# A decoder block that streams its weights: pieces split three ahead, with two raw buffers and 28 units

## The chip, the cores and the metric

The kernel runs on one core of a Trainium2 chip. The metric is the device time of one execution, in microseconds (us). A core has a matrix engine (TensorE, PE in the profile, with PEld for its weight loads), VectorE (DVE), ScalarE (ACT), GpSimd (POOL) and SyncE (SP), and 16 DMA engines that move data between the main memory and the on-chip memory. Each engine works through its own instructions in order and waits for the others by semaphores. In the profile SPq is the queue on which SyncE issues transfers.

## The reference

One decoder block over 256 tokens of width 2048, in float32. Cut to what matters:

```python
h = rms_norm(x, g_mix)
proj = h @ w_in                       # retention, dilated attention and their gates
merged = sigmoid(gate_ret) * (ret @ w_br_ret) + sigmoid(gate_dil) * (dil @ w_br_dil)
x = x + merged @ w_out
x = x + memory_cross_attention(rms_norm(x, g_cross), rms_norm(mem, g_mem), w_q_mem, w_kv_mem, w_o_mem)
hf = rms_norm(x, g_ffn)
# PEER: 16 of 16384 experts for each of 8 heads and each token
a = gelu(einsum('td,tkd->tk', hf, peer_u[idx]))
x = x + einsum('tk,tkd->td', a * gates, peer_v[idx])
out = rms_norm(x, g_final)
```

## The kernel before

All weights come from the main memory as 464 pieces of 1 MiB (128 partitions x 4 x 512 floats), in one fixed order. Pieces 0 to 99 are `w_in`, then follow the weights of the branches, of the output, of the cross attention and of the expert queries up to piece 207; pieces 208 to 335 are the table `u` of the experts and pieces 336 to 463 the table `v`. The experts are not gathered for most tokens: for 192 of the 256 tokens the kernel multiplies with the whole tables, weighted by a gate matrix G that it builds in the main memory. For the other 64 tokens it gathers rows of `u` and `v` (`lanes`, line 835) and works on them with VectorE (lines 843 and 861).

A float32 product is made of three products of a rounded high part and a low part. So each piece is loaded into a raw buffer (line 1167, issued by SyncE), ScalarE rounds it to the high part `hi` (line 1177), and VectorE subtracts to get the low part `lo` (line 1178). TensorE then multiplies with `hi` and `lo` (`mm3`, lines 210 to 212, and lines 916, 917, 1026, 1027): 24 products of 512 columns for a piece up to 207, 20 for a later one.

The order of the instructions is the order of the program text; nothing is reordered. `ahead(n)` stands before the work on piece n and splits all pieces up to n + SPLIT_AHEAD; behind each split it issues the load that reuses the raw buffer just read. The high and low parts have three buffers each (pool `stream`), the raw pieces three (RAW_BUFS), so the parts of piece n + 2 go into the buffers of piece n - 1, and the raw piece i + 3 into the buffer of piece i.

All other work is cut into generators that advance by `tick()` between the products: transposes, attention, the choice of the experts, the gate matrix (`gate_matrix`), the gathered rows (`lanes`), and `weigh`, which loads the gate rows and activations of a chunk of experts five items ahead (lines 939 to 944, on the SP queue), multiplies them (VectorE, line 969), transposes them on TensorE (line 974), copies the high part out on ScalarE (lines 977, 981) and the low part on VectorE (lines 950, 955). `weigh` runs during the second half of the program.

Nearly everything else that is kept on chip lies in one pool `units` of 30 buffers of 4 KiB per partition: tiles of x, rows of activations, operands of the expert products, gathered rows. A new unit takes a free buffer and its first writer waits for the last reader of the tile that held it. The three pools that the change touches take 3 x 8 + 2 x 3 x 8 + 30 x 4 = 192 KiB per partition.

Of the kernel before, what the change touches and what calls it, by code (L numbers as in the profile page):

```python
# [20 lines left out]
KQ = 4  # L21
# [8 lines left out]
N_EXP = N_KEYS * N_KEYS  # L30
N_CH = N_EXP // 512
V_GROUPS = (4, 8, 8, 8, 4)
RAW_BUFS = 3
SPLIT_AHEAD = 2
N_UNITS = 30
LANES = slice(64, 128)
LOW = slice(0, 64)
TICK = 4.0
# [37 lines left out]
def block_kernel(ctx, tc, a, out):  # L76
    nc = tc.nc
    ctx.enter_context(tc.manual_schedule())
    cp = ctx.enter_context(tc.tile_pool(name="consts", bufs=1))
    st = ctx.enter_context(tc.tile_pool(name="stream", bufs=3))  # L80
    up = ctx.enter_context(tc.tile_pool(name="units", bufs=N_UNITS))
    wp = ctx.enter_context(tc.tile_pool(name="work", bufs=4))
    sp = ctx.enter_context(tc.tile_pool(name="small", bufs=2))
# [3 lines left out]
    def unit(shape, dt=F32):  # L87
        return up.tile([128] + shape, dt, tag="unit", name="unit")
# [83 lines left out]
    def split_sb(raw, gi, kq, ks=range(4), into=None):  # L172

        hi, lo = into or (unit([4, T], F32R), unit([4, T], F32R))
        for k in ks:
            g = gains[:, gi, 4 * kq + k:4 * kq + k + 1]
            nc.scalar.activation(hi[:, k], raw[:, k], AF.Copy, scale=g)
            nc.vector.scalar_tensor_tensor(lo[:, k], raw[:, k], g, hi[:, k], op0=OP.mult, op1=OP.subtract)
        return hi, lo
# [69 lines left out]
    x_T = [None] * KQ  # L249
    sm = {}  # L250

    def load_xT(kq):
        raw = unit([4, T])
        nc.sync.dma_start(raw, a["xT"][kq])
        return raw
# [899 lines left out]
    stream = [e for e in prog if e[0] is not None]  # L1155
# [3 lines left out]
    def quarters(i):  # L1159
        return [slice(k, k + 1) for k in range(KQ)] if i <= RAW_BUFS else [slice(0, KQ)]  # L1160

    def load_to(m):
        while at["load"] < min(m, len(stream)):
            i = at["load"]
            raws[i] = st.tile([128, KQ, 512], F32, name="raw", bufs=RAW_BUFS)
            for ks in quarters(i):
                nc.sync.dma_start(raws[i][:, ks], stream[i][0][:, ks])
            at["load"] += 1

    def ahead(n):  # L1170
        while at["split"] < min(n + SPLIT_AHEAD + 1, len(stream)):
            i = at["split"]
            load_to(i + RAW_BUFS)
            raw = raws.pop(i)
            hi, lo = st.tile([128, KQ, 512], F32R, name="hi"), st.tile([128, KQ, 512], F32R, name="lo")
            for ks in quarters(i):
                nc.scalar.copy(hi[:, ks], raw[:, ks])  # L1177
                nc.vector.tensor_sub(lo[:, ks], raw[:, ks], hi[:, ks])  # L1178
            parts[i] = (hi, lo)
            at["split"] += 1  # L1180
            load_to(i + 1 + RAW_BUFS)

    raw_x = []
    for i in range(RAW_BUFS):
        raw_x.append(load_xT(i))
        raws[i] = st.tile([128, KQ, 512], F32, name="raw", bufs=RAW_BUFS)
        for k in range(KQ):
            nc.sync.dma_start(raws[i][:, k], stream[i][0][:, k])
    at["load"] = RAW_BUFS
    raw_x.append(load_xT(3))  # L1190
    for i in range(RAW_BUFS):
        raw = raws.pop(i)
        hi, lo = st.tile([128, KQ, 512], F32R, name="hi"), st.tile([128, KQ, 512], F32R, name="lo")
# [6 lines left out]
        parts[i] = hi, lo  # L1200
        at["split"] = i + 1
        load_to(i + 1 + RAW_BUFS)
    x_T[3] = split_sb(raw_x[3], 0, 3)
    n = 0
    for ap, fn in prog:
        if ap is None:
# [99 lines left out]
```

## Time and profile before

| | us |
|---|---|
| runs shown: median of 3 (lowest to highest) | 2597.49 (2588.37 to 2598.75) |
| the profiled execution | 2592.94 |
| its span, from the first to the last instruction | 2591.0 |
| TensorE busy in the span | 2497.3 |
| VectorE busy | 1874.5 |
| ScalarE busy | 1256.3 |
| GpSimd busy | 553.0 |

The rows below are from the profiled execution. Times on the left of a row count from the start of the span. In a row of a group of instructions, what stands before the bar is the line, the engine, the operation, what is written and read, and the count; behind it are busy time and mean duration, then the engine's idle time just before these instructions and what ended most of it. TensorE's products overlap, so that one has a mean of 0.39 us though a new one starts every 0.23 us.

### The profile page before, as it was taken

How to read it: one execution, taken by the hardware profiler on the slowest of the kernel's cores; microseconds unless marked ns; L12 is line 12 of the kernel's file. 1: busy time of each engine (PE TensorE's matmuls, PEld its weight loads, DVE VectorE, ACT ScalarE, POOL GpSimd, SP SyncE). 2: the span in 40 equal slices, each digit the busy share in tenths (PEclk: the TensorE clock that was granted, in tenths of full speed). 3: DMA queues.
4: the chain of work that ended last, by engine and by line, in shares of the span. 5: the costliest groups of instructions: out<-in, count | busy, mean ns of one | idle time of the engine just before them, and what ended most of it. 6: DMA issues, size and time to landing. Idle time of an engine off the chain costs nothing.

```text
span 2591.0 us, 29643 instructions
## 1 busy us (share of the span) xinstructions
PE 2497.3 (96%) x11426; PEld 2062.8 (80%) x11426; DVE 1874.5 (72%) x2168; ACT 1256.3 (48%) x1302; POOL 553.0 (21%) x361
## 2 busy tenths in 40 slices
PE   9999999999999999999989989999999899998998
PEld 7888888888888888888867768887877787876886
DVE  7566545787564344456889998887779888898984
ACT  6434334443355443454544458885554344443444
POOL 0211110001100000000023332323334454443621
PEclk9999999999999999999999999999999999999999
DMA  8555555567666554465569889999999999999984
GB/s 293 193 182 169 189 187 176 190 212 268 211 241 214 183 176 145 164 216 175 200 236 357 303 287 342 361 355 359 383 357 376 348 403 357 400 385 343 380 344 154
DMA packets 160141, 700.50 MB, mean 270 GB/s; under 512 B 15968, under 2 KB 40576, under 8 KB 101120
## 3 DMA queue, kind: packets, MB, share of 16 engines
q1 hardware_dynamic: 110352, 531.18, 57.6%
q0 software_dynamic: 42736, 154.85, 15.7%
q10 hardware_dynamic: 6912, 12.59, 1.3%
q8 instruction: 89, 1.46, 0.2%
q14 instruction: 52, 0.43, 0.0%
HBM read 666.01 MB, written 31.98 MB: 269 GB/s over the span
## 4 chain that ended last, share of the span: by engine, by line
PE 65%; DVE 11%; DMA 6%; issue 2%; ACT 1%; POOL 0%; SPq 0%; ACTq 0%; DVEq 0%; POOLq 0%
PE acc L211 16%; PE acc L212 16%; PE acc L210 16%; DVE lo L1178 5%; PE acc L1026 3%; PE acc L1027 3%; PE acc L916 3%; PE acc L917 3%; DMA unit<-G 2%; DMA raw<-in_v_dram 2%; DVE unit L843 2%; PE sm L772 2%; DMA unit<-act 1%; PE tp L193 1%; PE sm L594 1%
## 5 line engine op out<-in xcount | busy, mean ns | idle before, releaser
L1178 DVE TENSOR_TENSOR lo<-raw,hi 128x2048 fp32r<-128x2048 f32 (+1 forms) x464 | 1059.5, 2285 | 534.5 <-ACT hi L1177 533.5
L1177 ACT CAST hi<-raw 128x2048 fp32r<-128x2048 f32 (+1 forms) x464 | 880.2, 1900 | 665.9 <-PE acc L212 288.8
L211 PE MATMUL acc<-lo,unit 128*128 128x512 f32 x2688 | 1055.9, 393 | 33.9 <-DVE lo L1178 33.1
L210 PE MATMUL acc<-hi,unit 128*128 128x512 f32 x2688 | 1065.6, 396 | 6.5 <-ACT hi L1197 6.5
L212 PE MATMUL acc<-hi,unit 128*128 128x512 f32 x2688 | 1052.2, 391 | 0.0
L211 PEld LDWEIGHTS acc<-lo,unit 128*128 128x128 f32 x2688 | 508.2, 189 | 148.2 <-DVE lo L1178 47.4
L210 PEld LDWEIGHTS acc<-hi,unit 128*128 128x128 f32 x2688 | 508.0, 189 | 107.8 <-ACT hi L1197 7.0
L212 PEld LDWEIGHTS acc<-hi,unit 128*128 128x128 f32 x2688 | 507.8, 189 | 105.5
L835 POOL DMA_INDIRECT unit<-in_u_rows_dram,unit x128 | 216.4, 1691 | 446.8 <-DVE unit L843 157.6
L835 POOL DMA_INDIRECT unit<-in_v_rows_dram,unit x128 | 230.6, 1801 | 253.6 <-DVE unit L861 161.9
L1026 PE MATMUL acc<-hi,unit 128*128 128x512 f32 x512 | 201.7, 394 | 0.0
L1027 PE MATMUL acc<-lo,unit 128*128 128x512 f32 x512 | 201.3, 393 | 0.0
L916 PE MATMUL acc<-hi,unit 128*128 128x512 f32 x512 | 201.0, 393 | 0.0
L917 PE MATMUL acc<-lo,unit 128*128 128x512 f32 x512 | 200.6, 392 | 0.0
L861 DVE SCALAR_TENSOR_TENSOR unit<-unit 128x1024 f32<-128x1024 f32 x128 | 161.9, 1279 | 7.2 <-DMA unit<-xs 6.7
L843 DVE CUSTOM_DVE_ANT_0 unit<-unit 128x1024 f32<-128x1024 f32 x128 | 155.8, 1218 | 0.7 <-DMA unit<-in_u_rows_dram,unit 0.5
L1026 PEld LDWEIGHTS acc<-hi,unit 128*128 128x128 f32 x512 | 97.5, 190 | 21.1 <-DVE unit L955 0.2
L1027 PEld LDWEIGHTS acc<-lo,unit 128*128 128x128 f32 x512 | 97.4, 190 | 20.8
L916 PEld LDWEIGHTS acc<-hi,unit 128*128 128x128 f32 x512 | 97.3, 190 | 20.9
L917 PEld LDWEIGHTS acc<-lo,unit 128*128 128x128 f32 x512 | 97.1, 190 | 20.9
L342 POOL TENSOR_TENSOR unit<-work 128x512 f32<-128x512 f32 x20 | 37.7, 1884 | 176.4 <-DVE work L340 157.1
L169 POOL TENSOR_TENSOR rstd<-rstd2t,nhalf 128x2 f32<-128x2 f32 x1 | 0.7, 695 | 338.2 <-DVE rstd2t L163 338.2
(235 smaller groups left out, 1437.6 us busy)
## 6 DMA issues: line engine op xcount, KB each, us to landing
raw<-in_u_dram SPq DMA_DIRECT2D x128, 1024.0 KB, 6.9
raw<-in_v_dram SPq DMA_DIRECT2D x128, 1024.0 KB, 8.1
raw<-in_w_in_dram SPq DMA_DIRECT2D x96, 1024.0 KB, 4.9
raw<-in_w_kv_dram SPq DMA_DIRECT2D x32, 1024.0 KB, 4.9
raw<-in_w_out_dram SPq DMA_DIRECT2D x16, 1024.0 KB, 4.9
raw<-in_w_qm_dram SPq DMA_DIRECT2D x16, 1024.0 KB, 4.9
raw<-in_w_om_dram SPq DMA_DIRECT2D x16, 1024.0 KB, 4.9
raw<-in_w_pq_dram SPq DMA_DIRECT2D x16, 1024.0 KB, 4.9
```

What stands on the lines that cost most here:

```text
L210: nc.tensor.matmul(acc, lh, rh, start=start, stop=False)
L211: nc.tensor.matmul(acc, lh, rl, start=False, stop=False)
L212: nc.tensor.matmul(acc, ll, rh, start=False, stop=stop)
L835: nc.gpsimd.indirect_dma_start(rows[i], None, t, bass.IndirectOffsetOnAxis(ap=ix[:, j // 2, j % 2:j % 2 + 1], axis=0))
L843: nc.vector.tensor_tensor_reduce(r, r, hn[i % 2].rearrange("p a b -> p (a b)"), 1.0, 0.0, OP.mult, OP.add, dots[:, i // 2, i % 2:i % 2 + 1])
L861: nc.vector.scalar_tensor_tensor(y, r, coef[:, i // 2:i // 2 + 1], y, op0=OP.mult, op1=OP.add)
L916: nc.tensor.matmul(accs[1], th[:, k, 128:256], hi[:, k], start=first, stop=False)
L917: nc.tensor.matmul(accs[1], th[:, k, 128:256], lo[:, k], start=False, stop=last)
L1026: nc.tensor.matmul(accs[n][1], tb[:, k], hi[:, k], start=f, stop=False)
L1027: nc.tensor.matmul(accs[n][1], tb[:, k], lo[:, k], start=False, stop=e)
L1177: nc.scalar.copy(hi[:, ks], raw[:, ks])
L1178: nc.vector.tensor_sub(lo[:, ks], raw[:, ks], hi[:, ks])
```

## The change

The high and low parts get four buffers each and are made three pieces ahead; the raw pieces get two buffers, and the pool of units 28. The three pools take 2 x 8 + 2 x 4 x 8 + 28 x 4 = 192 KiB per partition, as before. At the start, two pieces and two tiles of x are loaded in turn, then the other two tiles of x, and these two are split behind the first two pieces.

```diff
-RAW_BUFS = 3
-SPLIT_AHEAD = 2
-N_UNITS = 30
+RAW_BUFS = 2
+SPLIT_AHEAD = 3
+N_UNITS = 28
@@
-    st = ctx.enter_context(tc.tile_pool(name="stream", bufs=3))
+    st = ctx.enter_context(tc.tile_pool(name="stream", bufs=SPLIT_AHEAD + 1))
@@
     at["load"] = RAW_BUFS
-    raw_x.append(load_xT(3))
+    raw_x.extend(load_xT(i) for i in range(RAW_BUFS, KQ))
     for i in range(RAW_BUFS):
         raw = raws.pop(i)
         hi, lo = st.tile([128, KQ, 512], F32R, name="hi"), st.tile([128, KQ, 512], F32R, name="lo")
@@
-    x_T[3] = split_sb(raw_x[3], 0, 3)
+    for i in range(RAW_BUFS, KQ):
+        x_T[i] = split_sb(raw_x[i], 0, i)
     n = 0
     for ap, fn in prog:
```

## Rows read from the trace of the kernel before

**Rows 1.** Busy time of the engines by stretch: span, PE, PEld, DVE, ACT, POOL, clock, DMA share, GB/s.
```profile
65.00:1242.00 1177.00, 1175.61 (x5458) 980.23 (x5457) 678.51 (x655) 510.33 (x515) 90.82 (x85) 1.00 0.56 193
1242.00:1546.00 304.00, 272.39 (x1151) 215.26 (x1150) 285.39 (x546) 144.66 (x122) 74.45 (x44) 0.98 0.79 284
1546.00:1799.00 253.00, 246.66 (x1279) 210.75 (x1278) 207.73 (x334) 210.02 (x337) 67.75 (x42) 0.99 0.97 347
1799.00:1942.00 143.00, 140.88 (x622) 116.09 (x621) 113.55 (x109) 74.61 (x60) 51.37 (x30) 0.99 0.99 372
1942.00:2371.00 429.00, 396.10 (x1765) 321.89 (x1764) 375.21 (x329) 176.13 (x135) 187.10 (x106) 0.97 1.00 376
2371.00:2484.00 113.00, 113.00 (x502) 93.58 (x502) 101.56 (x70) 49.28 (x30) 66.27 (x35) 1.00 0.96 372
```
**Rows 2.** The same stretches, VectorE's subtractions of line 1178 alone: busy time and count.
```profile
65.00:1242.00 1177.00, 457.27 (x199) 1.00 0.56 193
1242.00:1546.00 304.00, 128.48 (x57) 0.98 0.79 284
1546.00:1799.00 253.00, 100.76 (x44) 0.99 0.97 347
1799.00:1942.00 143.00, 68.74 (x30) 0.99 0.99 372
1942.00:2371.00 429.00, 184.05 (x81) 0.97 1.00 376
```
**Rows 3.** Groups of TensorE's instructions, the whole span: the two with most idle time.
```profile
L211 PE MATMUL acc<-lo,unit 128*128 128x512 f32 x2688 | 1055.9, 393 | 33.9 <-DVE lo L1178 33.1
...
L974 PE MATMUL tp<-ident,unit 128*128 128x128 f32 x192 | 32.0, 292 | 31.4 <-DVE unit L950 20.9 <-DVE unit L955 5.9 <-DVE unit L969 4.6
```
**Rows 4.** Timeline of ScalarE, 2387 to 2403 us: start, duration, instruction, idle time before.
```profile
2387.59 1.92 ACT L1177 CAST hi<-raw 128x2048 fp32r<-128x2048 f32 x1 [2.62 <-PE acc L1026]
2392.12 1.91 ACT L1177 CAST hi<-raw 128x2048 fp32r<-128x2048 f32 x1 [2.62 <-PE acc L1026]
```
**Rows 5.** Timeline of VectorE, 2387 to 2403 us.
```profile
2385.11 2.29 DVE L1178 TENSOR_TENSOR lo<-raw,hi 128x2048 fp32r<-128x2048 f32 x1
2387.32 1.28 DVE L861 SCALAR_TENSOR_TENSOR unit<-unit 128x1024 f32<-128x1024 f32 x1
2389.54 2.29 DVE L1178 TENSOR_TENSOR lo<-raw,hi 128x2048 fp32r<-128x2048 f32 x1 [0.94 <-ACT hi L1177]
```
**Rows 6.** Timeline of the SP queue, 2387 to 2403 us: three issues, from the first on.
```profile
2387.43 9.29 SPq L1167 DMA_DIRECT2D raw<-in_v_dram  x3
```
**Rows 7.** Raw loads from 65, 1242, 1546, 1799, 2484 us to the next.
```profile
DMA to landing us min/median/max: 4.7/4.9/10.6
...
DMA to landing us min/median/max: 4.7/5.5/9.8
...
DMA to landing us min/median/max: 4.7/7.9/11.8
...
DMA to landing us min/median/max: 4.8/8.2/14.5
...
DMA to landing us min/median/max: 4.8/5.1/9.0
```
**Rows 8.** Two single raw loads, issued at 2403.7 and 1354.6 us.
```profile
DMA to landing us min/median/max: 5.1/5.1/5.1
...
DMA to landing us min/median/max: 8.7/8.7/8.7
```
**Rows 9.** What ended the idle time before the splits, 1799 to 2591 us: us, times.
```profile
  DMA raw<-in_v_dram: 98.3, 35
```
**Rows 10.** The row gathers of line 835, 1990 to 2500 us, and their engine's waits.
```profile
L835 POOL DMA_INDIRECT unit<-in_v_rows_dram,unit x128: 932/1737/3942, 2005.0 to 2484.5; - x128
...
  DVE unit L861: 161.9, 70
...
DMA to landing us min/median/max: 4.8/10.2/16.5
```

## The prediction

> **What bounds the kernel now.** I read the busy time by stage first [rows 1], with the number of splits in each stage [rows 2]; then what TensorE waits for [rows 3]; then one turn of the raw buffers on ScalarE, VectorE and the DMA queue [rows 4 to 6]; then how long the loads take in each stage [rows 7, 8]; last what ends the waits of the splits, and the row gathers [rows 9, 10].
>
> TensorE is the bound nearly everywhere. From 65 to 1242 us it is busy 1175.6 of 1177 us, and from 2371 to 2484 all the time. Its idle time lies in three stages [rows 1]: 304 - 272.4 = 31.6 us from 1242 to 1546, 253 - 246.7 = 6.3 us up to 1799, and 429 - 396.1 = 32.9 us from 1942 to 2371. Of all its idle time only 33.9 us end with a split that came late (the second product of a piece needs the low part); 31.4 us more end with a transpose that waits for VectorE's work on the tile before it [rows 3]. A third piece split ahead can help with the first sum alone: TensorE works in order, and a transpose that waits is not passed by pieces that lie ready.
>
> The stage from 1242 to 1546 has a second limit, VectorE, busy 285.4 of 304 us (94%). From 1799 to 2371 the DMA engines have work 99 to 100% of the time [rows 1], and 35 splits there start late because their raw piece has not landed [rows 9]: 98.3 us of ScalarE's idle time. These cost little today because the parts lie ready early. TensorE frees a buffer, and so changes to the next piece, every 2392.12 - 2387.59 = 4.53 us [rows 4]. The conversion of 2387.59 ends at 2389.51, the subtraction behind it at 2389.54 + 2.29 = 2391.83 [rows 5], and the piece is wanted two changes after the one at 2387.59: 2387.59 + 9.06 - 2391.83 = 4.8 us later.
>
> **The change, part by part.** (1) *The place of the split.* Before piece n the program now splits piece n + 3, with four buffers, and not n + 2, with three. Both wait for the same event, the end of piece n - 1 on TensorE. So the order on ScalarE, VectorE and the SP queue stays as it is, one piece further on; the load that follows the split is that of piece n + 5 before and after, in the same place of the queue. Each piece's parts then lie ready one period earlier: 4.53 us in the late stages. The number of conversions and subtractions is the same.
>
> (2) *Two raw buffers.* The load of a piece waits for the subtraction of the piece that held its buffer: it ends at 2385.11 + 2.29 = 2387.40 us, and the queue issues at 2387.43 [rows 5, 6]. That was the piece three before; it will be the piece two before. One turn of a buffer is the load, the conversion (1.92), the subtraction (2.29) and two hand-overs (0.03 each): landing time L plus 4.27 us. With three buffers there are 3 x 4.53 = 13.59 us for it, so L may be 9.3 us; with two there are 9.06 us, and L may be 4.8. The queue holds the raw loads of later pieces behind this wait, and the loads of gate rows and activations for the second half, so they move with it. Who waits: the conversion on ScalarE, behind it the copies that drain transposes, and the subtraction on VectorE with all that is queued there.
>
> L by stage today [rows 7]: median 4.9, 5.5, 7.9, 8.2 and 5.1 us, never under 4.7. Part of the 8.2 us is waiting behind another raw load: 8.2 / 4.53 = 1.8 of them are in flight at once. With two buffers that is 2L / (L + 4.5), or 1.1 at L = 6, so the queue ahead nearly goes. The price of a load alone beside gathers is not shown as such; two loads that were issued with no other raw load in flight bound it, 5.1 and 8.7 us [rows 8]. From the other side: 8.2 is 4.8 plus 3.4 for 0.8 of a load ahead; 0.1 of a load leaves 4.8 + 0.4 = 5.2. Between 5.2 and the middle of the two rows, 6.9, I take 6.0 where gathers and the loads of gates run, 5.5 where gathers run alone, 4.8 behind them. For the splitting part I take 4.5 us (4.27 and a little for other work in VectorE's order).
>
> Stage by stage, two buffers giving (L + 4.5) / 2 us a piece:
> - 65 to 1242: 1177 / 199 = 5.9 us a piece [rows 1, 2] against (4.9 + 4.5) / 2 = 4.7. Hidden under TensorE's own work; the cover is 1.2 us a piece, and L may reach 7.3 before it is used up. 0.
> - 1242 to 1546: 304 / 57 = 5.3 us, against (5.5 + 4.5) / 2 = 5.0. The lead on entry rises by a piece, but VectorE has only 6% to spare and eats the lead as before. The gain is at most the 25 us of waits that lie here, the loss at most (9.8 - 6.2) / 2 = 1.8 us for each of 57 loads if all were as slow as the slowest. I take 0.
> - 1546 to 1799: 253 / 44 = 5.75 us, against (6.0 + 4.5) / 2 = 5.25; with L = 7.9 unchanged it is 6.2, or 20 us. I take +5, nearer the end where the queue ahead is gone.
> - 1799 to 1942: 30 pieces, 4.53 against 5.25: +22.
> - 1942 to 2371: 81 pieces in 429 us; without the 32.9 us of idle time 4.89 each. 5.25 x 81 = 425, and the waits for gates and activations hold up VectorE, and so the splits, as they do now; I leave 28 of the 32.9: 453, or +24.
> - 2371 to 2484: 113 / 4.53 = 25 pieces, (5.5 + 4.5) / 2 = 5.0: +12. After 2484: (4.8 + 4.27) / 2 = 4.53: 0.
> - The parts that lie ready on entering the late stages are used up first: 4.8 + 4.53 = 9.3 us of delay that TensorE does not feel: -9.
>
> Sum: 5 + 22 + 24 + 12 - 9 = +54 us.
>
> By the Trainium skill (DMA: Bandwidth & Descriptors, "Anatomy of one DMA"), which gives about 2 us fixed plus the bytes at 436 GB/s, for loads issued by GpSimd, an estimate for 1 MiB is 4.4 us, and a turn would be 8.7 us, inside the 9.06. No load in [rows 7] is that short, so the sum goes by the rows.
>
> (3) *28 units and not 30.* In the steady groups of the second half the program before hands the gathered rows five buffers in turn (its buffer assignment repeats with every fifth row); two fewer leave three. A gather for row i + 3 then waits for the work on row i, and no longer for that on row i - 2. Already 70 of the waits on GpSimd end there [rows 10]. Free if the gather still lands in time: between 0 and the price of the rival below. I take 0, and the price into the range.
>
> (4) *The start.* The third raw piece is loaded behind the first split and two tiles of x, and piece 3 no longer in quarters. The nearest row is a load of 4.9 us [rows 7]; between -1 and +5 us, taken as 0, for TensorE still works on the two pieces before.
>
> The profiled execution takes 2592.9 us (span 2591.0 and 1.9 around it); 2592.9 + 54 = 2647. The median of the runs shown is 4.6 us above the profiled one; I put the forecast between 2647 and 2652, at 2650.
>
> **The rivals.** *Two buffers are enough.* If L falls to 4.8 once no raw load stands ahead of another, a turn takes 9.06 us and the late stages keep 4.53. For it: 4.8 is the shortest landing in the late stages, gathers or not. Against it: gathers and gate loads share the engines, and the two single loads took 5.1 and 8.7. Time: 2597, no change.
> The Trainium skill's page Trainium Kernel Development and Optimization says under "Best Practices" to "Double-buffer for performance"; by that rule this rival would hold. The trace before has three buffers everywhere and can't show it; its 35 splits that wait for a landing [rows 9] speak against it.
>
> *The lead wins.* Under the same condition (L up to 4.8 in the late stages, up to 6.1 from 1242 to 1546) the third piece ahead takes away most of the 33.9 us that TensorE waits for low parts: 25 us at most, since VectorE stays at 94%. For it: L is 5.5 in that stage. Against it: the same as above for the late half. Time: 2597 - 25 = 2572, and it decides as soon as the landings stay under these bounds.
>
> *The units are too few.* A gather lands 10.2 us after its issue (median, up to 16.5), one every (2484.5 - 2005.0) / 128 = 3.75 us [rows 10]. Issued behind row i, it is wanted 3 x 3.75 - 1.28 [rows 5] = 10.0 us later: half of them would be late, and VectorE, with the splits behind it, waits. At 0.4 us each on 128 rows that is 50 us on top: 2700. Against it: three gathers in flight and not five land sooner.
>
> **How the numbers follow.** The raw buffers limit the late half: 0.56, 2612 to 2700. With too few units on top: 0.20, 2660 to 2780. Two buffers enough: 0.13. The lead wins: 0.11. The likeliest gives 2650. The range from 2590 to 2730 takes in no change; it leaves out the fast case and the upper part of the units. A measurement of this kernel can tell about 0.5%, 13 us. Faster 0.11, same 0.13, slower 0.76.
>
> **What would show it.** The splits in the late stages should wait for landings far more than 35 times, with each issue 0.03 us behind the subtraction two pieces before; L should fall to 5 to 6.5 us, the DMA share below 0.99, and the period from 1799 to 2484 rise from 4.53 to about 5.2 us, with TensorE idle in every piece. Up to 1242 nothing should move. It is wrong if the period stays at 4.53 us or L under 4.9; if VectorE waits for gathered rows, the units have decided.

## The result and the profile after

The changed kernel takes 2749.4 us (median of 4 runs, 2744.42 to 2753.83), the kernel before 2595.9 us: the ratio is 1.0603, with a 95% interval from 1.0585 to 1.0622. It is 154 us slower. The direction was forecast, the size was not: 2650 us, with a range that ended at 2730.

The profiled execution of the changed kernel took 2753.8 us. Its page begins with the busy time:

```profile
PE 2541.1 (92%) x11426; PEld 2077.3 (75%) x11426; DVE 1876.5 (68%) x2165; ACT 1255.6 (46%) x1299; POOL 497.6 (18%) x361
```

VectorE and ScalarE are busy as long as before (within 2 us), GpSimd is busy 55 us less; TensorE is busy for 92% of a longer span, and for 44 us more. The next view is the busy time by stretch, cut at the same pieces as [rows 1] (columns as there; the last stretch has no counterpart among those rows):

```profile
65.00:1253.00 1188.00, 1177.97 (x5457) 981.48 (x5456) 681.58 (x665) 517.28 (x523) 93.37 (x86) 1.00 0.56 193
1253.00:1576.00 323.00, 275.97 (x1152) 218.01 (x1152) 287.75 (x549) 145.70 (x122) 69.68 (x44) 0.95 0.76 268
1576.00:1849.00 273.00, 253.08 (x1278) 213.82 (x1278) 207.38 (x330) 208.56 (x337) 59.53 (x41) 0.97 0.93 320
1849.00:2017.00 168.00, 144.92 (x618) 114.81 (x617) 113.83 (x110) 73.73 (x60) 45.19 (x31) 0.97 0.86 317
2017.00:2502.00 485.00, 413.31 (x1778) 329.44 (x1777) 375.62 (x329) 176.85 (x137) 164.31 (x107) 0.94 0.92 331
2502.00:2629.00 127.00, 117.31 (x489) 93.61 (x487) 93.39 (x64) 44.53 (x28) 48.22 (x33) 0.96 0.86 310
2629.00:2740.00 111.00, 100.10 (x419) 78.90 (x419) 70.47 (x47) 49.80 (x44) 14.69 (x13) 0.98 0.60 222
```

Against [rows 1] the stages grow by 11, 19, 20, 25, 56 and 14 us, and the rest after 2629 us by 16: (2751.9 - 2629) - (2591.0 - 2484). Together that is the whole difference of the spans, 161 us. The loss lies in every stage from the second on (the second begins with piece 208, its loss with piece 228), and a little at the start. The DMA engines are less busy than before (0.86 to 0.93 where it was 0.96 to 1.00), and VectorE has a smaller share of each stage. So neither bandwidth nor an engine became the bound; something waits in a circle.

TensorE's two groups with waits, as in [rows 3]:

```profile
L211 PE MATMUL acc<-lo,unit 128*128 128x512 f32 x2688 | 1065.6, 396 | 78.6 <-DVE lo L1178 78.1
...
L974 PE MATMUL tp<-ident,unit 128*128 128x128 f32 x192 | 33.2, 300 | 67.0 <-DVE unit L950 60.8 <-DVE unit L969 3.6 <-DVE unit L955 2.5
```

The waits for low parts are 78.6 us and not 33.9, and the transposes wait 67.0 us and not 31.4: VectorE stands before a subtraction whose piece has not landed, with the work for the transposes behind it. What ends the idle time before the splits, from 1849 us to the end (us, times), answers to [rows 9]:

```profile
  DMA raw<-in_v_dram: 310.8, 88
...
  DMA raw<-in_u_dram: 69.0, 22
```

110 of 153 conversions there wait for a landing; before it was 39 of 154 (the 35 of [rows 9] and 4 of the table `u`). One turn on VectorE, the SP queue and ScalarE (timelines; start, duration, instruction; the queue's row stands for four issues from the first on):

```profile
1942.26 2.29 DVE L1178 TENSOR_TENSOR lo<-raw,hi 128x2048 fp32r<-128x2048 f32 x1 [2.78 <-ACT hi L1177]
```
```profile
1944.58 15.10 SPq L1167 DMA_DIRECT2D raw<-in_u_dram  x4
```
```profile
1945.87 1.91 ACT L1177 CAST hi<-raw 128x2048 fp32r<-128x2048 f32 x1 [3.02 <-DMA raw<-in_u_dram]
...
1949.44 1.91 ACT L1177 CAST hi<-raw 128x2048 fp32r<-128x2048 f32 x1 [1.66 <-DMA raw<-in_u_dram]
```

The subtraction ends at 1942.26 + 2.29 = 1944.55, the queue issues the next load of that buffer at 1944.58, and ScalarE has idle time before each conversion until the piece lands. The landing times of the raw loads from 65, 1253, 1576, 1849 and 2629 us on, as [rows 7]:

```profile
DMA to landing us min/median/max: 4.7/4.9/9.3
...
DMA to landing us min/median/max: 4.7/5.4/8.7
...
DMA to landing us min/median/max: 4.8/7.0/10.1
...
DMA to landing us min/median/max: 4.7/6.9/12.2
...
DMA to landing us min/median/max: 4.7/4.9/8.6
```

They fell, from 8.2 to 6.9 us in the late stages, but not to the 6.0 and 5.5 of the forecast.

The turn can be measured for every piece: from the issue of its load to the end of its subtraction. These are means over all raw loads of a stage of the changed kernel, worked out from its trace (us):

| pieces | landing | held, landing to end of subtraction | half a turn | measured period | half a turn in the forecast |
|---|---|---|---|---|---|
| 228 to 263 | 6.25 | 5.44 | 5.85 | 5.89 | 5.0 |
| 264 to 307 | 6.93 | 5.06 | 6.00 | 6.20 | 5.25 |
| 308 to 337 | 6.68 | 4.83 | 5.76 | 5.60 | 5.25 |
| 338 to 419 | 6.99 | 4.92 | 5.96 | 5.99 | 5.25 |
| 420 to 443 | 6.58 | 5.17 | 5.87 | 5.26 | 5.0 |
| 444 to 462 | 5.82 | 4.64 | 5.23 | 5.22 | 4.53 |

But for one stage half a turn is the measured period within 0.2 us. From 420 to 443 TensorE still used up pieces that lay ready when the stretch began.

This agreement alone does not show that the buffers set the pace. A raw buffer is loaded again 0.03 us behind its subtraction, so the turn divided by the number of buffers comes out as the period in any steady stretch. In the kernel before a third of the mean turn is 5.26 us from piece 338 to 419, and the period 5.34 us; there the holding time (6.74 us) also holds the wait for TensorE. What tells the two kernels apart is how long a piece lies landed before its conversion starts. In the stages from piece 264 on the means are 1.8 to 4.2 us before (loads whose landing the trace has) and 0.3 to 0.8 us after. Before, a landed piece waited for its turn on the engines; now the engines wait for the piece.

### The profile page after: what moved, and what is told of

Same layout as the page of the kernel before. It is cut to its first block, busy times and chain, and to the rows that moved or that the text cites. A ratio compares the mean times of both kernels' runs of the same rounds, so it can differ in the third digit from the quotient of the medians.

```text
span 2751.9 us, 29687 instructions
## 1 busy us (share of the span) xinstructions
PE 2541.1 (92%) x11426; PEld 2077.3 (75%) x11426; DVE 1876.5 (68%) x2165; ACT 1255.6 (46%) x1299; POOL 497.6 (18%) x361
## 4 chain that ended last, share of the span: by engine, by line
PE 39%; DMA 22%; DVE 16%; ACT 6%; issue 5%; POOL 1%; ACTq 0%; SPq 0%; DVEq 0%; POOLq 0%
DMA raw<-in_v_dram 11%; PE acc L210 11%; PE acc L212 11%; PE acc L211 11%; DVE lo L1178 9%; DMA raw<-in_u_dram 9%; ACT hi L1177 6%; DVE unit L843 1%; DVE unit L861 1%; PE tp L193 1%; PE sm L772 1%; PE acc L916 1%; DMA unit<-in_v_rows_dram,unit 1%; PE sm L594 1%; PE sm L625 1%
## 5 line engine op out<-in xcount | busy, mean ns | idle before, releaser
L211 PE MATMUL acc<-lo,unit 128*128 128x512 f32 x2688 | 1065.6, 396 | 78.6 <-DVE lo L1178 78.1
L835 POOL DMA_INDIRECT unit<-in_u_rows_dram,unit x128 | 196.9, 1538 | 537.6 <-DVE unit L843 244.3
L835 POOL DMA_INDIRECT unit<-in_v_rows_dram,unit x128 | 194.8, 1522 | 357.2 <-DVE unit L861 254.3
L1027 PE MATMUL acc<-lo,unit 128*128 128x512 f32 x512 | 204.7, 400 | 0.0
L917 PE MATMUL acc<-lo,unit 128*128 128x512 f32 x512 | 202.3, 395 | 0.0
L974 PE MATMUL tp<-ident,unit 128*128 128x128 f32 x192 | 33.2, 300 | 67.0 <-DVE unit L950 60.8
L974 PEld LDWEIGHTS tp<-ident,unit 128*128 128x128 f32 x192 | 24.5, 152 | 79.5 <-DVE unit L950 67.3
```

The costliest lines, as they stand in the source:

```text
L211: nc.tensor.matmul(acc, lh, rl, start=False, stop=False)
L835: nc.gpsimd.indirect_dma_start(rows[i], None, t, bass.IndirectOffsetOnAxis(ap=ix[:, j // 2, j % 2:j % 2 + 1], axis=0))
L917: nc.tensor.matmul(accs[1], th[:, k, 128:256], lo[:, k], start=False, stop=last)
L1027: nc.tensor.matmul(accs[n][1], tb[:, k], lo[:, k], start=False, stop=e)
```

## The experiments

Each kernel was timed beside the kernel before on the same chip (2594 to 2598 us). In the runs without gathers the rows of `u` and `v` for 64 tokens are not fetched but filled with zeros on chip.

### Which of the three parts costs

**Two raw buffers alone** (two pieces ahead, 30 units):

```diff
-RAW_BUFS = 3
+RAW_BUFS = 2
```

The start is that of the changed kernel.

> Two raw buffers alone; pieces split two ahead with three buffers for the parts, 30 units. If the turn of the raw buffers carries the loss, this takes nearly all of it: 2720 to 2760 us, with the late stages at 5.2 to 6.0 us a piece and most splits there starting at a landing. If the units carry a good part, it stays under 2700. If the third piece ahead softens the loss, it is 10 to 30 us slower than the changed kernel, over 2760.

Measured: 2765.4 us, ratio 1.0654 (1.0624 to 1.0685), 171 us slower. The raw buffers alone bring more than the whole loss. The time lies 5 us over the range expected, where the third theory stood (the third piece ahead softens the loss); the run with two raw buffers and 28 units, below, speaks against that theory.

**28 units alone:**

```diff
-N_UNITS = 30
+N_UNITS = 28
```

> 28 units alone; three raw buffers, two pieces ahead. If the raw buffers carry the loss: 2590 to 2605 us, no difference that can be told. If too few units carry part of it, by gathers that are issued two rows later: 2630 to 2660, with VectorE waiting for gathered rows in the second half.

Measured: 2656.4 us, ratio 1.0237 (1.0219 to 1.0254), 62 us slower. This is what the rival on the units said. VectorE's work on the rows of `v`, which waited 0.5 us for rows in the kernel before, has this row (group, and the idle time just before it):

```profile
L861 DVE SCALAR_TENSOR_TENSOR unit<-unit 128x1024 f32<-128x1024 f32 x128 | 163.5, 1280 | 95.6 <-DMA unit<-in_v_rows_dram,unit 92.6 <-DMA unit<-xs 2.9
```

92.6 us of waits for rows, and all of the loss lies from 1941 us on, where these rows are used: up to there its pieces start at the same times as in the kernel before, within 1 us.

**29 units:**

```diff
-N_UNITS = 30
+N_UNITS = 29
```

> 29 units, otherwise as before. The gathered rows then turn over four buffers, not five (30 units) or three (28). If a gather lands in time when it is issued behind the row two before (wanted some 11 us after a landing time of 10): 2595 to 2610 us. If the loss grows evenly with each unit: about 2625.

Measured: 2596.6 us, ratio 1.0012 (0.9998 to 1.0026). The loss does not grow evenly: one buffer fewer is free, the second costs 62 us. The same row in this run:

```profile
L861 DVE SCALAR_TENSOR_TENSOR unit<-unit 128x1024 f32<-128x1024 f32 x128 | 162.8, 1279 | 28.9 <-DMA unit<-in_v_rows_dram,unit 22.2 <-DMA unit<-xs 6.6
```

22.2 us of late rows cost no time that can be told; 92.6 us do.

**Two raw buffers and 28 units**, without the third piece ahead (the edit is against the changed kernel; the parts have three buffers):

```diff
-SPLIT_AHEAD = 3
+SPLIT_AHEAD = 2
```

> Two raw buffers and 28 units, but pieces split two ahead with three buffers for the parts: the changed kernel without the third piece ahead. If the raw buffers carry the loss alone: within 10 us of the run with two raw buffers. If the third piece ahead gains something: 10 to 30 us slower than the changed kernel (2760 to 2780). If it costs something, for instance at the start: faster than 2745.

Measured: 2748.7 us, ratio 1.0590 (1.0572 to 1.0608). That is the changed kernel's time, 2749.4. So with two raw buffers the third piece ahead gains nothing and costs nothing in sum. TensorE's waits for low parts are 107.4 us without it and 78.6 with it, but those of its transposes of lines 974, 739 and 193 are 62.0 us without it and 93.7 with it: the waits move. And the two other parts do not add: 171 and 62 us alone, 154 together. With two raw buffers TensorE's pace is so slow that the rows come in time (the changed kernel's row):

```profile
L861 DVE SCALAR_TENSOR_TENSOR unit<-unit 128x1024 f32<-128x1024 f32 x128 | 162.0, 1278 | 6.8 <-DMA unit<-in_v_rows_dram,unit 4.9 <-DMA unit<-xs 1.9
```

That 28 units even make two raw buffers 17 us faster goes with shorter landings from piece 264 to 337: 7.0 and 6.6 us on average, against 7.2 and 6.9 with 30. Fewer gathers in flight beside a load would explain that, but the traces do not show them: while a raw load of these pieces was on its way, 1.26 and 1.34 gathers were in flight on average with 28 units, 1.18 and 1.34 with 30. The cause of these 17 us stays open.

**Four raw buffers, 28 units:**

```diff
-RAW_BUFS = 3
+RAW_BUFS = 4
-N_UNITS = 30
+N_UNITS = 28
```

At the start four pieces and all four tiles of x are loaded in turn, and three pieces are split, as before.

> The other way: four raw buffers, 28 units, two pieces ahead (the same room on the chip as both kernels). If the raw turn limits the late half even with three buffers (35 splits there wait for a landing): 2560 to 2590 us. If the waits for landings are covered by the pieces that lie ready: 2590 to 2600. If 28 units cost something: over 2605.

Measured: 2650.7 us, ratio 1.0214 (1.0197 to 1.0232), 6 us less than with 28 units and three raw buffers. With 28 units a fourth raw buffer is worth little. That the 35 waits for landings in the kernel before [rows 9] were covered follows only if 30 units behave alike; four raw buffers with 30 units were not run. The kernel before with split halves, below, points the same way.

### What the gathers have to do with it

```diff
-                nc.gpsimd.indirect_dma_start(rows[i], None, t, bass.IndirectOffsetOnAxis(
-                    ap=ix[:, j // 2, j % 2:j % 2 + 1], axis=0))
+                nc.gpsimd.memset(rows[i], 0.0)
```

**The kernel before without gathers:**

> The kernel before with the gathers of the rows left out (each row is filled with zeros on chip instead; VectorE's work on it stays). It is the reference for the three runs beside it. Gathers compete for the DMA engines but the kernel before covers that: 2560 to 2595 us.

Measured: 2556.5 us, a little better than expected. The kernel before took 2597.6 us beside it, so the gathers cost it 41 us.

**The changed kernel without gathers:**

> The changed kernel with the gathers left out in the same way. If the turn of two raw buffers is the limit and gathers only lengthen the landings: landings of 4.8 to 5.5 us from piece 308 to 338, 4.6 to 4.9 us a piece there, and a loss of 40 to 90 us against the run without gathers beside it, not 154. If the loss hangs on gathers that come late: no loss.

Measured: 2619.1 us, 63 us slower than the run above. From piece 308 to 337 the landings are as expected (loads issued from 1764 to 1917 us):

```profile
DMA to landing us min/median/max: 4.8/5.2/7.1
```

The period there is 5.02 us, more than the 4.6 to 4.9 expected: the mean turn is 10.15 us, half of it 5.08. So the change costs 63 us even without gathers, and the rest goes with landings that are longer beside gathers (6.68 us on average from piece 308 to 337, and 5.43 without). Of the 63 us, 12 arise before piece 14 (below), 5 up to piece 263, 11 from 264 to 337 and 34 behind.

**28 units without gathers:**

> 28 units without gathers, otherwise as before. If 28 units cost time only by gathers that are issued late (VectorE waited 93 us for rows in the run with 28 units alone): within 8 us of the kernel before without gathers. If the other writers of units wait too (gate rows, transposed copies): 20 to 60 us slower.

Measured: 2558.9 us, 2 us more than the kernel before without gathers. With 28 units only the gathers come late; the other writers of units lose nothing that can be told.

**Three pieces ahead with three raw buffers**, in 26 units, without gathers (the parts have four buffers):

```diff
-SPLIT_AHEAD = 2
+SPLIT_AHEAD = 3
-N_UNITS = 30
+N_UNITS = 26
-ROWS_AHEAD = 3
+ROWS_AHEAD = 1
```

> Three pieces ahead with three raw buffers, which has room only with 26 units; they suffice without gathers and with rows one ahead. It shows the third piece ahead by itself. If it is worth the waits for late low parts: 10 to 30 us faster than the kernel before without gathers. If TensorE's waits lie elsewhere (transposes, and a VectorE that is full): within 8 us of it.

Measured: 2573.1 us, 16.5 us slower than the kernel before without gathers; neither theory said that. The trace has the place: 14 us arise between pieces 80 and 85, in the dilated attention, where a transposed tile has to wait for a unit that a store of gates still reads (who waited for whom from 478 to 545 us: us, times, longest):

```profile
ACT unit L483 <- DMA gate_r<-unit: 13.9, 2, 7.2
...
PE sm L488 <- ACT unit L483: 6.6, 2, 3.6
```

The trace so puts it down to the 26 units and not to the third piece; 26 units with two pieces ahead were not run. From piece 86 to the end this kernel is within 2 us of the run without it, though TensorE's waits for low parts fell by 10 us, from 25.2 to

```profile
L211 PE MATMUL acc<-lo,unit 128*128 128x512 f32 x2688 | 1052.8, 392 | 15.2 <-DVE lo L1175 14.9
```

The third piece ahead does what it says, and TensorE then waits elsewhere: six transposes of line 739, between 1340 and 1550 us, wait 15.7 us for VectorE's work, and 5.3 without the third piece.

```profile
L739 PE MATMUL tp<-ident,unit 128*128 128x128 f32 x6 | 1.9, 349 | 15.7 <-DVE unit L732 11.5 <-DVE unit L719 4.2
```

### Two runs on the turn, and the opposite

**The changed kernel with splits in two halves:**

```diff
-            for ks in quarters(i):
+            for ks in quarters(i) if i <= RAW_BUFS else (slice(0, 2), slice(2, 4)):
                 nc.scalar.copy(hi[:, ks], raw[:, ks])
                 nc.vector.tensor_sub(lo[:, ks], raw[:, ks], hi[:, ks])
```

> The changed kernel with each split made in two halves: ScalarE rounds the first half and VectorE subtracts it while ScalarE rounds the second. A raw buffer is then held about 3.5 us and not 4.4, at the price of two more instructions a piece. If the turn (landing time and holding time, halved) sets the pace behind piece 228, each of some 235 pieces gains up to 0.45 us: 2650 to 2700 us, less where gathers come late again. If the pace hangs on DMA bandwidth or on late gathers: 2740 to 2755.

Measured: 2708.2 us, ratio 1.0431 (1.0400 to 1.0462): 41 us less than the changed kernel, though VectorE is busy 36 us longer (1912.2 and not 1876.5). The direction tells the theories apart, the size is under the expectation. The holding time fell by 0.8 us from piece 308 to 337 (4.83 to 4.03), but the landings rose by 0.56 (6.68 to 7.24), as more loads are issued while the other is still on its way (26 of 30 with more than 0.3 us of it outstanding, and not 21). The turn became 0.26 us shorter there, 0.78 us from piece 420 to 443 and 0.55 us behind.

**The kernel before with the same halves:**

> The kernel before with the same halves. Its three raw buffers already keep pace, so a shorter turn gains little, and the two more instructions a piece cost VectorE some 0.06 us each where it is full (1242 to 1546 us): 2585 to 2605 us. If the 35 splits that wait for a landing cost time: 2560 to 2585.

Measured: 2598.5 us, ratio 1.0020 (1.0002 to 1.0038). With three buffers a shorter turn gains nothing.

**One piece ahead, four raw buffers, 32 units:**

```diff
-RAW_BUFS = 3
-SPLIT_AHEAD = 2
-N_UNITS = 30
+RAW_BUFS = 4
+SPLIT_AHEAD = 1
+N_UNITS = 32
```

The pool `stream` gets SPLIT_AHEAD + 1 buffers, as in the changed kernel; at the start four pieces are loaded and two split.

> The opposite of the change in the same room: one piece ahead with two buffers for the parts, four raw buffers, 32 units. If what counts is raw buffers and units, and pieces split ahead are worth little: 2580 to 2610 us. If one piece ahead leaves TensorE waiting for low parts whenever VectorE is late by more than 0.3 us: over 2630.

Measured: 2716.5 us, ratio 1.0474 (1.0449 to 1.0500). TensorE's waits for low parts:

```profile
L211 PE MATMUL acc<-lo,unit 128*128 128x512 f32 x2688 | 1070.4, 398 | 118.7 <-DVE lo L1178 117.4
```

So the second piece ahead is worth some 120 us, if four raw buffers and 32 units by themselves cost nothing (not run), and the third none. Of the shares of this room that were tried, the kernel before has the best.

## Why the prediction was right in kind and wrong in size

**The mechanism was right.** The two raw buffers set the pace: the issue 0.03 us behind the subtraction, the splits that wait for landings (110 and not 39), a period over 5.2 us, all as forecast. Two raw buffers alone give the loss; a shorter turn gives part of it back. "Two buffers are enough" and "the lead wins" fell: the first by the 171 us, the second by the run with three pieces ahead and three raw buffers, which without gathers gained nothing.

**The landing time was mis-sized.** I took 6.0 us beside gathers, 5.5 after the gate loads, 4.8 at the end, on the step that "the queue ahead nearly goes". It measured 6.7 to 7.0, 6.6 and 5.8. From piece 308 to 419 the price of a load alone was not at fault: from 308 to 337 the 9 loads that were issued with at most 0.3 us of another raw load outstanding took 5.6 us, and from 338 to 419 the 26 of 82 took 6.0. The others took 7.2 and 7.5. (From 444 on the price was at fault as well: 9 such loads took 5.6 us, not 4.8.) The step counted how many loads are in flight on average, 1.1, and read the small excess over one as hardly any waiting. The average came out nearly so (2 x 6.99 / 11.91 = 1.17), but the subtractions that free the two buffers end 3.3 to 11.4 us apart, and two out of three loads start while the other is on its way. In the changed kernel without gathers the same two groups took 5.1 and 5.5 us from 338 to 419: most of the difference is there only beside gathers. The runs do not tell how much of it is waiting behind the other raw load and how much is gathers.

**The holding time was mis-sized too**: 4.5 us against 4.8 to 5.4, because other work in VectorE's and ScalarE's order stands between landing and subtraction. Together the two errors are 0.5 to 0.9 us a piece on 235 pieces; part of it was hidden where TensorE's own pace left room. By stage, the spans grew by 161 us and the forecast added up to 54. The 107 us between are 11 at the start, 19 from 1242 to 1546 us, 15, 3, 32 and 2 in the four stages up to 2484, 16 behind (put at 0), and the 9 us of lead that were taken off.

**The stage from 1242 to 1546 was put at 0 and cost 19 us.** Here I used the median landing of the stage (5.5 us) and a holding time of 4.5. The loss begins with piece 228. From there to 263 the mean landing is 6.25 and, where VectorE is full, the holding time 5.44: half a turn is 5.85 us, over the 5.37 that these pieces took before. The stage's median [rows 7] hid this: in the kernel before, the 20 loads up to piece 227 took 5.2 us on average and the later ones 6.4.

**The start was put at 0, with 5 us as its upper end, and cost 11 us.** TensorE's cover was there for the pieces, not for the rest. The rows of x for the sum of squares (line 263) are loaded on the same SP queue, and each of these loads stands behind a raw load that waits for its buffer. The forecast had seen this for the loads of gates and activations and left out the start. The first of them in the kernel before, then in the changed kernel (timelines of the queue, 36 to 56 us):

```profile
36.72 0.42 SPq L263 DMA_DIRECT2D unit<-in_x_dram  x1
```
```profile
45.95 0.43 SPq L263 DMA_DIRECT2D unit<-in_x_dram  x1
```

ScalarE's first square of x then starts at 51.8 us and not 42.6, the step behind the sum (POOL, line 169) at 71.7 and not 62.4, and the first transposes wait for what hangs on it (group of TensorE's instructions, 74 to 98 us):

```profile
L193 PE MATMUL tp<-ident,unit 128*128 128x128 f32 x8 | 2.2, 435 | 8.7 <-POOL unit L342 8.7
```

The chain is read from the traces; a kernel with these loads elsewhere was not run.

**The units** were right as a mechanism and as a price (50 us forecast, 62 measured by themselves), but wrong in how they meet the first: I put the price on top. A slower pace gives each gather more time, so the two limits hide one another.

**The third piece ahead** was put at 9 us of delay that TensorE does not feel. It was worth nothing, with two raw buffers (2748.7 against 2749.4) and with three (without gathers). The forecast's own step held here: a transpose that waits is not passed by pieces that lie ready, and the waits for low parts became waits of transposes.

**The two places in the Trainium skill.** "Double-buffer for performance" (the Trainium skill, Trainium Kernel Development and Optimization, "Best Practices") says to overlap loads with work; it does not say that two buffers are enough. Read that way, as the rival did, it would have made the change free; here two raw buffers cost 171 us against three. The estimate of 4.4 us for a load (the Trainium skill, DMA: Bandwidth & Descriptors, "Anatomy of one DMA", a fit for loads issued by GpSimd) is under the shortest load in any trace here, 4.6 us, and far under the mean of 6.7 to 7.0 in the late stages.

## What to carry to other kernels

A buffer that is filled, read and filled again sets a pace of its own: landing time plus holding time, divided by the number of buffers. Put in the holding time without what a landed piece waits for the bound engine, the means of stretches in which the loads are alike, and let the landings keep what they wait behind one another; then compare with the pace of the bound engine. From piece 338 to 419 that pace was 5.34 us before. Three buffers were enough: a landing of 8.9 us before and a holding time of 4.9, as in the changed kernel, make 13.8 us, or 4.6 a piece (an estimate). Two were not: 11.9 us, or 6.0 a piece. Before buffers are moved from one pool to another, find for each pool the number at which its loop just keeps pace: 29 units were free and 28 cost 62 us, two pieces ahead were worth 120 us and the third nothing.

## What was not expected of the hardware

Here TensorE pays for its waits a second time. In the changed kernel it stood still for 8.7 us between 81 and 92, with only eight transposes in these 11 us; around this the profile shows (busy time by stretch, columns as in [rows 1]; the granted clock is the third number from the end):

```profile
76.00:81.00 5.00, 5.00 (x23) 3.90 (x21) 2.29 (x1) 2.28 (x2) 5.00 (x4) 1.00 0.61 223
81.00:84.00 3.00, 0.10 (x1) 0.00 (x0) 2.27 (x2) 0.70 (x1) 1.37 (x1) 1.00 0.79 306
84.00:94.00 10.00, 4.20 (x14) 3.42 (x15) 5.11 (x8) 4.41 (x4) 4.51 (x2) 0.50 0.61 210
```

From 84 us on the granted clock is 0.50 (the 1.2 GHz level) and not 1.00 (2.4 GHz), and it stays so for some time after the products begin again. Over the whole span 187 products of the changed kernel ran at the lower level, 0.43 us apart and not 0.23; in the kernel before 82 did. The difference, 105 x 0.2 = 21 us, is part of the 44 us by which TensorE's busy time grew (2497.3 to 2541.1) and stood in no term of the forecast. How much of it shows in the time cannot be told, for in these stages TensorE waits in any case.
